# One order of products in all weight tiles of a pair, and all activation slots in one stretch of SBUF beside the split weights

## The chip, the cores and the metric

One NeuronCore of one Trainium2 chip. The metric is the device time of one execution in microseconds, the median of three runs. The profile is that of one further execution of the same program.

## What is computed

A two-layer encoder on 256 positions of 2048 channels. Layer 0 mixes by a conformer convolution module, layer 1 by differential attention; each is followed by a feed-forward network (FFN) with 5632 hidden channels and a short causal convolution in it. Everything is float32.

```python
for i in range(DEPTH):                                     # DEPTH = 2
    h = _rmsnorm(x, mix_norm[i])
    m = _conformer_conv(h, ...) if i % 2 == 0 else _diff_attention(h, ...)
    x = x + m
    h = _rmsnorm(x, ffn_norm[i])
    x = x + _conv_ffn(h, ffn_w_up[i], ffn_dw_w[i], ffn_dw_b[i], ffn_w_down[i])
return _rmsnorm(x, final_norm_g)

def _conv_ffn(h, w_up, dw_w, dw_b, w_down):
    u = _causal_dwconv(h @ w_up, dw_w, dw_b)
    gate, val = jnp.split(u, 2, axis=-1)
    return (jax.nn.silu(gate) * val) @ w_down
```

## The kernel before

Channels lie on the 128 partitions and the 256 positions along the free axis. Every matrix is walked in **pairs**: two column blocks of 128 outputs each (`j` = 0, 1), accumulated over all input blocks `k` of 128 channels into one PSUM tile of two banks (pool `pp`, two buffers, so that one pair is evacuated while the next is computed). Weights come by DMA on SP's queue in tiles of 128x1024 (four `k` of a pair, 512 KB) into pool `rawp`. `split_w` makes two tiles of each: `hi`, a rounded copy by ScalarE (L160), and `lo`, the rest, by VectorE or GpSimd (L164). An activation tile holds the same two parts side by side, 128x2x256.

`pair` issues, for each `k` and each `j`, two products on TensorE: **main**, the `hi` weights with both parts of the activation (512 columns), and **corr**, the `lo` weights with the activation's upper part (256 columns, added to the second half of the same bank). For all `k` but the last the order is main, corr (L249, L250); for the last `k` of a pair it is corr, main (L246, L247). One main with its corr is called a **duo** below; a pair over 16 `k` has 32 duos. A pair of FFN's `w_up` has 16 `k`; one of `w_down` has 8 (4 in the first of its chunks). `merged` pairs (the conv module's `w_in`, and the last pair of each `w_down`) use another form, three products of 256 columns (L240). When a pair is done, `post` sums the two halves and works on them on ScalarE and VectorE.

Activation tiles are slots of 2 KB a partition. `act_tile` gives them out of pool `acta` (25 slots) as long as it has one free, and after that out of `actb` (8 slots). The pools lie in SBUF in the order in which they are opened: `const`, `rawp`, `hip`, `lop`, `acta`, `sm`, and then `ph1`, which holds what only the convolution module needs. When `acta` first runs out, `ph1` is closed, and `ph2` (attention's tiles) and `actb` are laid over it. So the slots of `acta` lie behind the weight tiles at multiples of 2 KB, and those of `actb` 44,512 bytes behind the end of `acta`, which is no multiple of 64 bytes (32 over).

TensorE's order of instructions is fixed when the program is built. A planner runs through the program with modelled times and puts an instruction where its inputs are ready, by the order of the source among those that are. Between the duos come small blocks of other products: the norm's channel sums (`chan_sums`, L297, four of 2 columns) and its row broadcast (`rows`, L303, four of 128 columns), each once per norm, a few duos before and after a pair's end early in the FFN; the attention's scores, transposes and value products (L952, L977, L987, L1005) in the pairs of its heads; and single products of the bias table and of lambda (L839, L857) in the first FFN's first two pairs. Within an FFN no other block comes after the row broadcast, up to its last, merged pair. In `w_o` the first two pairs hold back their last `k` until attention's last head is done (`held`), so that the next pair begins without the swapped order there.

Of the kernel before, what the change touches and what calls it, by code (L numbers as in the profile page):

```python
# [8 lines left out]
F32 = mybir.dt.float32  # L9
# [5 lines left out]
P = 128  # L15
S = 256
# [3 lines left out]
FK = 3  # L20
# [5 lines left out]
class Cfg:  # L26


    def __init__(self, d, f, kc=4):
        self.D, self.F = d, f  # L30
        self.KT = d // P
        self.FT = f // P
        self.H = d // (2 * HD)
        self.KC = kc
        self.NW = kc * 256
        self.kcs = [(i, kc) for i in range(0, self.KT, kc)]
        full = self.KT // 2
        first = self.FT % full or full
        self.chunks = [(0, first)] + [(i, full) for i in range(first, self.FT, full)]
        self.VK = kc // 2  # L40
        self.NA, self.NB = self.KT + self.KT // 2 + 1, 8

        self.G = [3] * (self.KT - 3) + [5, 6, 0]

        self.ND = 16
# [16 lines left out]
class Builder:  # L62
    def __init__(self, ctx, tc, cfg, a):
        self.tc, self.nc, self.c, self.a = tc, tc.nc, cfg, a
        ec = ctx.enter_context
        self.ctx = ctx
        self.const = ec(tc.tile_pool(name="const", bufs=1))
        self.rawp = ec(tc.tile_pool(name="rawp", bufs=5))
        self.hip = ec(tc.tile_pool(name="hip", bufs=6))
        self.lop = ec(tc.tile_pool(name="lop", bufs=6))  # L70
        self.acta = ec(tc.tile_pool(name="acta", bufs=cfg.NA))
        self.sm = ec(tc.tile_pool(name="sm", bufs=2))
        self.pp = ec(tc.tile_pool(name="pp", bufs=2, space=bass.MemoryType.PSUM))
        self.px = ec(tc.tile_pool(name="px", bufs=1, space=bass.MemoryType.PSUM))
        self.dr = ec(tc.tile_pool(name="dr", bufs=1, space=bass.MemoryType.DRAM))
        self.ph1_stack = ExitStack()
        self.ph1 = self.ph1_stack.enter_context(tc.tile_pool(name="ph1", bufs=2))
        self.actb = None
        self.na, self.nb = cfg.NA, 0
        self.coloff, self.ncol = cfg.cols()  # L80
        self.steps, self.W, self.todo = [], [], {}
        self.s = self.n = self.np_ = self.ns = 0
        self.every = self.pool_first = None
# [4 lines left out]


    def b2(self, tag, dt=F32):  # L90
        return self.sm.tile([P, 2, S], dt, tag=tag, name=self.nm(tag), bufs={"E": 4, "Y": 4, "Z": 2, "A": 2}[tag])

    def b1(self, tag):
        return self.sm.tile([P, S], F32, tag=tag, name=self.nm(tag), bufs={"G": 4, "O": 3, "M": 3}[tag])
# [17 lines left out]


    def act_tile(self, dt=F32R):
        if self.na > 0:
            self.na -= 1
            return ("a", self.acta.tile([P, 2, S], dt, tag="act", name=self.nm("act")))
        if self.actb is None:
            self.ph1_stack.close()
            self.ph2 = self.ctx.enter_context(self.tc.tile_pool(name="ph2", bufs=1))  # L120
            self.actb = self.ctx.enter_context(self.tc.tile_pool(name="actb", bufs=self.c.NB))
            self.nb = self.c.NB
        assert self.nb > 0
        self.nb -= 1
        return ("b", self.actb.tile([P, 2, S], dt, tag="actb", name=self.nm("actb")))

    def free(self, tiles):
        for w, _ in tiles:
            if w == "a":
                self.na += 1  # L130
            else:
                self.nb += 1


    def load_w(self):
# [90 lines left out]
    def pair(self, wsrc, off, ksub, src, post, lo="v", pre=None, held=None, merged=False, halves=None):  # L226


        nc = self.nc
        box = {}  # L230
        first, last = ksub[0][0], ksub[-1][0] + ksub[-1][1] - 1

        def one(hi, lo_, kk, k):
            xt = src(k)[1]
            for j in range(2):
                ps = box["ps"][j] if halves else box["ps"][:, j, :]
                cs = slice(j * P, (j + 1) * P)
                if merged:
                    for n, (w, x) in enumerate(((hi, 0), (hi, 1), (lo_, 0))):
                        nc.tensor.matmul(ps[:, 0:S], w[:, kk, cs], xt[:, x, :], start=(k == first and n == 0),  # L240
                                         stop=(k == last and n == 2))
                    continue
                main = (ps, hi[:, kk, cs], xt.rearrange("p a s -> p (a s)"))
                corr = (ps[:, S:], lo_[:, kk, cs], xt[:, 0, :])
                if k == last:
                    nc.tensor.matmul(*corr, start=False, stop=False)  # L246
                    nc.tensor.matmul(*main, start=False, stop=True)  # L247
                else:
                    nc.tensor.matmul(*main, start=(k == first), stop=False)  # L249
                    nc.tensor.matmul(*corr, start=False, stop=False)  # L250

        for si, (k0, nk) in enumerate(ksub):
            n = nk * 256
            w = wsrc[off:off + P * n].rearrange("(p n) -> p n", p=P)
            off += P * n

            def mm(hi, lo_, k0=k0, nk=nk, si=si):
                if si == 0:
                    box["ps"] = halves() if halves else self.pp.tile([P, 2, 512], F32, tag="pp", name=self.nm("pp"))
                for kk in range(nk):  # L260
                    if held is not None and k0 + kk == last:
                        box["w"] = (hi, lo_, kk, last)
                    else:
                        one(hi, lo_, kk, k0 + kk)

            end = si == len(ksub) - 1
            self.step(w, n, 256, mm, post=(lambda: post(box["ps"])) if end and held is None else None,
                      pre=pre if si == 0 else None, lo=lo[si % len(lo)])
        if held is not None:
            held.append((lambda: one(*box["w"]), lambda: post(box["ps"])))  # L270
        return off
# [139 lines left out]
    def setup(self, n0):  # L411
        nc, c, a = self.nc, self.c, self.a
# [25 lines left out]
        with self.tc.manual_schedule(engines={ET.DVE, ET.Activation, ET.Pool}):  # L438
            for m in range(KT):
                if m in (0, 2):  # L440

                    first = self.split_w() if m == 0 else first
# [12 lines left out]

        self.todo[7] = [lambda: self.norm_cols(n0)]
        self.todo[8] = [lambda: self.norm_rows(n0)]
        self.fpad = []
        for i in range(2):
            t = self.const.tile([P, 2, S + FK - 1], F32, name=f"fpad{i}")  # L460
            nc.vector.memset(t[:, :, 0:FK - 1], 0.0)
            self.fpad.append(t)
        self.cpad = []
        for i in range(4):
            t = self.ph1.tile([P, S + CK + 1], F32, name=f"cpad{i}", bufs=1)
# [5 lines left out]
    def conv_module(self, nin, nout):  # L471
        c, a = self.c, self.a
# [197 lines left out]
        def layernorm():  # L670
# [24 lines left out]
            nc.vector.tensor_tensor(mr, mean, rc, ALU.mult)  # L695

            rp = [self.psx("s", [P, S]) for _ in range(2)]
            rs = self.b2("E")
            for x, v in enumerate((rc, mr)):
                self.rows(rp[x], v)  # L700
# [129 lines left out]
    def attn_setup(self):  # L830

        nc, c, a = self.nc, self.c, self.a
        H = c.H
        rb = self.ph2.tile([NB, H], F32, name="rb")
        self.tc.keep_in_program_order(nc.gpsimd.dma_start(rb, a["relb"]))
        oh = self.b2("Z").rearrange("p a s -> p (a s)")[:NB, :384]
# [327 lines left out]
```

## Time and profile before

| | |
|---|---|
| median of 3 runs | 2229.67 us (2228.4 to 2231.36) |
| the profiled execution | 2228.45 us |
| its span, first to last instruction | 2226.7 us |
| granted TensorE clock over the span | 0.997 |

How to read it: the span is what the trace covers; 1.75 us of the profiled execution's time lie around it. The profiled execution is 1.2 us below the median. A timeline row gives the start and the length of one instruction (or of a run of like ones, `x4`), its engine, its line and its tiles, output before the arrow. Matmuls are pipelined, so that a row's length reaches over the start of the next; what a product costs in a stream is the distance between two starts. Starts are given to 0.01 us, so a cadence is read over several duos. A windows row gives a stretch, its length, the busy time and the number of instructions of TensorE's matmuls, its weight loads, VectorE, ScalarE and GpSimd in it, and then TensorE's granted clock, the DMA share and GB/s.

### The profile page before, as it was taken

How to read it: one execution, taken by the hardware profiler on the slowest of the kernel's cores; microseconds unless marked ns; L12 is line 12 of the kernel's file. 1: busy time of each engine (PE TensorE's matmuls, PEld its weight loads, DVE VectorE, ACT ScalarE, POOL GpSimd, SP SyncE). 2: the span in 40 equal slices, each digit the busy share in tenths (PEclk: the TensorE clock that was granted, in tenths of full speed). 3: DMA queues.
4: the chain of work that ended last, by engine and by line, in shares of the span. 5: the costliest groups of instructions: out<-in, count | busy, mean ns of one | idle time of the engine just before them, and what ended most of it. 6: DMA issues, size and time to landing. Idle time of an engine off the chain costs nothing.

```text
span 2226.7 us, 34566 instructions
## 1 busy us (share of the span) xinstructions
PE 2202.7 (99%) x13274; PEld 1935.3 (87%) x13274; DVE 1629.1 (73%) x2482; ACT 1200.9 (54%) x1799; POOL 251.1 (11%) x175
## 2 busy tenths in 40 slices
PE   9999899999999999999999999999999999999998
PEld 8899788888888888888888888888888888888887
DVE  5888777787767677677687778767777677776774
ACT  5333555555555455555565555555555455554554
POOL 2987510000000000000100000100000000000002
PEclk9999999999999999999999999999999999999999
DMA  7876365666666656665655555556666566666652
GB/s 262 229 221 199 115 189 184 196 200 196 198 197 200 189 189 186 191 187 186 194 171 182 171 171 172 173 188 189 188 185 189 188 189 189 190 189 189 189 188 97
DMA packets 127317, 417.15 MB, mean 187 GB/s; under 512 B 14608, under 2 KB 28576, under 8 KB 127152
## 3 DMA queue, kind: packets, MB, share of 16 engines
q1 hardware_dynamic: 115584, 403.32, 58.2%
q10 hardware_dynamic: 11472, 11.54, 2.1%
q8 instruction: 104, 1.70, 0.3%
q14 instruction: 61, 0.50, 0.1%
q0 software_dynamic: 96, 0.08, 0.0%
HBM read 410.13 MB, written 7.33 MB: 187 GB/s over the span
## 4 chain that ended last, share of the span: by engine, by line
PE 95%; issue 2%; DVE 1%; POOL 1%; DMA 1%; ACT 0%; POOLq 0%; ACTq 0%
PE pp L249 49%; PE pp L250 25%; PE pp L240 6%; PE pp L247 4%; PE pp L246 2%; PE pp L900 1%; PE pp L902 1%; PE pp L901 1%; PE s L952 1%; PE s L542 1%; DMA R<-ud 1%; PE o L987 0%; POOL lo L164 0%; PE s L249 0%; DVE s L599 0%
## 5 line engine op out<-in xcount | busy, mean ns | idle before, releaser
L249 PE MATMUL pp<-act,hi 128*128 128x512 f32 x3902 | 1378.7, 395 | 1.6 <-ACT hi L160 1.1
L250 PE MATMUL pp<-act,lo 128*128 128x256 f32 x3902 | 1095.0, 281 | 0.0
L164 DVE TENSOR_TENSOR lo<-raw,hi 128x1024 fp32r<-128x1024 f32 (+1 forms) x693 | 849.8, 1228 | 286.7 <-ACT hi L160 285.2
L160 ACT CAST hi<-raw 128x1024 fp32r<-128x1024 f32 (+1 forms) x753 | 788.0, 1047 | 499.8 <-PE pp L249 190.9
L249 PEld LDWEIGHTS pp<-act,hi 128*128 128x128 f32 x3902 | 731.6, 187 | 161.5 <-ACT hi L160 1.4
L250 PEld LDWEIGHTS pp<-act,lo 128*128 128x128 f32 x3902 | 737.1, 189 | 9.8
L249 PE MATMUL pp<-actb,hi 128*128 128x512 f32 x856 | 306.9, 396 | 0.0
L250 PE MATMUL pp<-actb,lo 128*128 128x256 f32 x856 | 240.3, 281 | 0.0
L347 POOL TENSOR_TENSOR ssq<-ssq,Z 128x512 f32<-128x512 f32 x24 | 35.9, 1496 | 1549.1 <-ACT Z L343 1549.0
L249 PEld LDWEIGHTS pp<-actb,hi 128*128 128x128 f32 x856 | 160.6, 188 | 38.4 <-issue 0.6
L240 PE MATMUL pp<-act,hi 128*128 128x256 f32 x1024 | 188.5, 286 | 3.1 <-ACT act L290 1.9
L240 PEld LDWEIGHTS pp<-act,hi 128*128 128x128 f32 x1024 | 160.7, 193 | 9.4 <-issue 4.9
L277 ACT COPY E<-pp 128x512 f32<-128x512 f32 x104 | 60.9, 586 | 190.1 <-PE pp L247 190.1
L250 PEld LDWEIGHTS pp<-actb,lo 128*128 128x128 f32 x856 | 161.5, 189 | 0.2
L402 ACT COPY E<-pp 128x512 f32<-128x512 f32 x109 | 63.9, 586 | 170.3 <-PE pp L247 162.6
L279 DVE TENSOR_TENSOR E<-pp,E 128x512 f32<-128x512 f32 x104 | 71.9, 691 | 111.5 <-ACT E L277 111.5
L788 DVE SCALAR_TENSOR_TENSOR Y<-fpad,prm,Y 128x256 f32<-128x256 f32 x352 | 146.7, 477 | 0.0
L240 PE MATMUL pp<-act,lo 128*128 128x256 f32 x512 | 145.4, 284 | 0.3 <-DVE lo L164 0.3
L164 POOL TENSOR_TENSOR lo<-raw,hi 128x1024 fp32r<-128x1024 f32 x60 | 142.8, 2406 | 14.3 <-ACT hi L160 7.3
L404 DVE TENSOR_TENSOR x<-pp,x 128x512 f32<-128x512 f32 x101 | 69.7, 690 | 87.8 <-ACT E L402 87.4
L785 ACT ACTIVATE Y<-fpad,prm 128x256 f32<-128x256 f32 x176 | 96.3, 595 | 45.5 <-DVE fpad L781 45.5
L599 DVE SCALAR_TENSOR_TENSOR s<-cpad,cprm,s 128x256 f32<-128x256 f32 x182 | 85.2, 486 | 20.2 <-PE s L542 16.8
(214 smaller groups left out, 1846.9 us busy)
## 6 DMA issues: line engine op xcount, KB each, us to landing
raw<-in_w_up_dram SPq DMA_DIRECT2D x352, 512.0 KB, 3.7
raw<-in_w_down_dram SPq DMA_DIRECT2D x176, 512.0 KB, 3.7
raw<-in_w_qk_dram SPq DMA_DIRECT2D x64, 512.0 KB, 3.6
raw<-in_w_in_dram SPq DMA_DIRECT2D x63, 512.0 KB, 4.8
raw<-in_w_out_dram SPq DMA_DIRECT2D x32, 512.0 KB, 3.8
raw<-in_w_v_dram SPq DMA_DIRECT2D x32, 512.0 KB, 3.7
raw<-in_w_o_dram SPq DMA_DIRECT2D x32, 512.0 KB, 3.7
R<-ud ACTq DMA_DIRECT2D x52, 132.0 KB, 5.9
```

The costliest lines, as they stand in the source:

```text
L160: nc.scalar.copy(hi[:, p], raw[:, p])
L164: ins = eng.tensor_tensor(lo[:, p], raw[:, p], hi[:, p].bitcast(F32), ALU.subtract)
L240: nc.tensor.matmul(ps[:, 0:S], w[:, kk, cs], xt[:, x, :], start=(k == first and n == 0), stop=(k == last and n == 2))
L247: nc.tensor.matmul(*main, start=False, stop=True)
L249: nc.tensor.matmul(*main, start=(k == first), stop=False)
L250: nc.tensor.matmul(*corr, start=False, stop=False)
L279: nc.vector.tensor_tensor(t, ps[:, :, 0:S], cs, ALU.add)
L402: nc.scalar.copy(cs, ps[:, :, S:])
L404: nc.vector.tensor_tensor(x, ps[:, :, 0:S], x, ALU.add)
L599: nc.vector.scalar_tensor_tensor(acc, u[:, j:j + S], self.col("cw", i * CK + j), acc, ALU.mult, ALU.add)
L785: nc.scalar.activation(y[:, j, :], u[:, j, FK - 1:], AF.Identity, scale=self.col("fw", ch * FK + FK - 1), bias=self.col("fb", ch))
L788: nc.vector.scalar_tensor_tensor(y[:, j, :], u[:, j, q:q + S], self.col("fw", ch * FK + q), y[:, j, :], ALU.mult, ALU.add)
```

## The change

- `pair` issues main, then corr for every `k`, the last one too.
- `actb` is gone: `acta` has 33 slots (the 25 and the 8), and the pools are opened in the order `const`, `hip`, `lop`, `acta`, `rawp`, `sm`.
- To make room, the tiles E and A of `sm` and the two `fpad` tiles of `const` move to `ph2`. `ph2` is opened by the new function `second`, called in the conv module's layernorm before its E tile (`rs`). `fpad` is made in `attn_setup`, and its two small memsets run on GpSimd in place of VectorE.

```diff
@@ -38,7 +38,7 @@
         first = self.FT % full or full
         self.chunks = [(0, first)] + [(i, full) for i in range(first, self.FT, full)]
         self.VK = kc // 2
-        self.NA, self.NB = self.KT + self.KT // 2 + 1, 8
+        self.NA = self.KT + self.KT // 2 + 9
 
         self.G = [3] * (self.KT - 3) + [5, 6, 0]
 
@@ -65,18 +65,19 @@
         ec = ctx.enter_context
         self.ctx = ctx
         self.const = ec(tc.tile_pool(name="const", bufs=1))
-        self.rawp = ec(tc.tile_pool(name="rawp", bufs=5))
+
         self.hip = ec(tc.tile_pool(name="hip", bufs=6))
         self.lop = ec(tc.tile_pool(name="lop", bufs=6))
         self.acta = ec(tc.tile_pool(name="acta", bufs=cfg.NA))
+        self.rawp = ec(tc.tile_pool(name="rawp", bufs=5))
         self.sm = ec(tc.tile_pool(name="sm", bufs=2))
         self.pp = ec(tc.tile_pool(name="pp", bufs=2, space=bass.MemoryType.PSUM))
         self.px = ec(tc.tile_pool(name="px", bufs=1, space=bass.MemoryType.PSUM))
         self.dr = ec(tc.tile_pool(name="dr", bufs=1, space=bass.MemoryType.DRAM))
         self.ph1_stack = ExitStack()
         self.ph1 = self.ph1_stack.enter_context(tc.tile_pool(name="ph1", bufs=2))
-        self.actb = None
-        self.na, self.nb = cfg.NA, 0
+        self.ph2 = None
+        self.na = cfg.NA
         self.coloff, self.ncol = cfg.cols()
         self.steps, self.W, self.todo = [], [], {}
         self.s = self.n = self.np_ = self.ns = 0
@@ -88,7 +89,8 @@
 
 
     def b2(self, tag, dt=F32):
-        return self.sm.tile([P, 2, S], dt, tag=tag, name=self.nm(tag), bufs={"E": 4, "Y": 4, "Z": 2, "A": 2}[tag])
+        pool = self.ph2 if tag in "EA" else self.sm
+        return pool.tile([P, 2, S], dt, tag=tag, name=self.nm(tag), bufs={"E": 4, "Y": 4, "Z": 2, "A": 2}[tag])
 
     def b1(self, tag):
         return self.sm.tile([P, S], F32, tag=tag, name=self.nm(tag), bufs={"G": 4, "O": 3, "M": 3}[tag])
@@ -112,24 +114,17 @@
 
 
     def act_tile(self, dt=F32R):
-        if self.na > 0:
-            self.na -= 1
-            return ("a", self.acta.tile([P, 2, S], dt, tag="act", name=self.nm("act")))
-        if self.actb is None:
-            self.ph1_stack.close()
-            self.ph2 = self.ctx.enter_context(self.tc.tile_pool(name="ph2", bufs=1))
-            self.actb = self.ctx.enter_context(self.tc.tile_pool(name="actb", bufs=self.c.NB))
-            self.nb = self.c.NB
-        assert self.nb > 0
-        self.nb -= 1
-        return ("b", self.actb.tile([P, 2, S], dt, tag="actb", name=self.nm("actb")))
+        assert self.na > 0
+        self.na -= 1
+        return ("a", self.acta.tile([P, 2, S], dt, tag="act", name=self.nm("act")))
 
     def free(self, tiles):
-        for w, _ in tiles:
-            if w == "a":
-                self.na += 1
-            else:
-                self.nb += 1
+        self.na += len(tiles)
+
+    def second(self):
+
+        self.ph1_stack.close()
+        self.ph2 = self.ctx.enter_context(self.tc.tile_pool(name="ph2", bufs=1))
 
 
     def load_w(self):
@@ -242,12 +237,8 @@
                     continue
                 main = (ps, hi[:, kk, cs], xt.rearrange("p a s -> p (a s)"))
                 corr = (ps[:, S:], lo_[:, kk, cs], xt[:, 0, :])
-                if k == last:
-                    nc.tensor.matmul(*corr, start=False, stop=False)
-                    nc.tensor.matmul(*main, start=False, stop=True)
-                else:
-                    nc.tensor.matmul(*main, start=(k == first), stop=False)
-                    nc.tensor.matmul(*corr, start=False, stop=False)
+                nc.tensor.matmul(*main, start=(k == first), stop=False)
+                nc.tensor.matmul(*corr, start=False, stop=(k == last))
 
         for si, (k0, nk) in enumerate(ksub):
             n = nk * 256
@@ -455,11 +446,6 @@
 
         self.todo[7] = [lambda: self.norm_cols(n0)]
         self.todo[8] = [lambda: self.norm_rows(n0)]
-        self.fpad = []
-        for i in range(2):
-            t = self.const.tile([P, 2, S + FK - 1], F32, name=f"fpad{i}")
-            nc.vector.memset(t[:, :, 0:FK - 1], 0.0)
-            self.fpad.append(t)
         self.cpad = []
         for i in range(4):
             t = self.ph1.tile([P, S + CK + 1], F32, name=f"cpad{i}", bufs=1)
@@ -695,6 +681,7 @@
             nc.vector.tensor_tensor(mr, mean, rc, ALU.mult)
 
             rp = [self.psx("s", [P, S]) for _ in range(2)]
+            self.second()
             rs = self.b2("E")
             for x, v in enumerate((rc, mr)):
                 self.rows(rp[x], v)
@@ -831,6 +818,11 @@
 
         nc, c, a = self.nc, self.c, self.a
         H = c.H
+        self.fpad = []
+        for i in range(2):
+            t = self.ph2.tile([P, 2, S + FK - 1], F32, name=f"fpad{i}")
+            nc.gpsimd.memset(t[:, :, 0:FK - 1], 0.0)
+            self.fpad.append(t)
         rb = self.ph2.tile([NB, H], F32, name="rb")
         self.tc.keep_in_program_order(nc.gpsimd.dma_start(rb, a["relb"]))
         oh = self.b2("Z").rearrange("p a s -> p (a s)")[:NB, :384]
```

## Rows read from the trace of the kernel before

**Rows 1.** Page, part 1: TensorE busy us, share of the span, instructions.

```profile
PE 2202.7 (99%) x13274; PEld 1935.3 (87%) x13274; DVE 1629.1 (73%) x2482; ACT 1200.9 (54%) x1799; POOL 251.1 (11%) x175
```

**Rows 2.** Timeline, a pair of the second w_up, then one of the first.

```profile
1496.88 0.39 PE L249 MATMUL pp<-act,hi 128*128 128x512 f32 x1
...
1505.55 0.39 PE L249 MATMUL pp<-actb,hi 128*128 128x512 f32 x1
...
660.12 0.39 PE L249 MATMUL pp<-actb,hi 128*128 128x512 f32 x1
...
664.34 0.28 PE L246 MATMUL pp<-actb,lo 128*128 128x256 f32 x1
...
665.04 0.40 PE L249 MATMUL pp<-act,hi 128*128 128x512 f32 x1
```

**Rows 3.** Timeline, first w_down: the last product of three pairs of 16 duos.

```profile
1000.10 0.40 PE L247 MATMUL pp<-act,hi 128*128 128x512 f32 x1
...
1005.66 0.39 PE L247 MATMUL pp<-act,hi 128*128 128x512 f32 x1
...
1011.30 0.40 PE L247 MATMUL pp<-act,hi 128*128 128x512 f32 x1
```

**Rows 4.** Timeline, w_out: the last product of pairs of 32 duos.

```profile
281.76 0.39 PE L247 MATMUL pp<-act,hi 128*128 128x512 f32 x1
...
292.87 0.39 PE L247 MATMUL pp<-act,hi 128*128 128x512 f32 x1
...
338.07 0.39 PE L247 MATMUL pp<-act,hi 128*128 128x512 f32 x1
```

**Rows 5.** Timeline, w_o: accumulator changes (pp, s) without a swapped order.

```profile
1401.14 0.40 PE L249 MATMUL pp<-act,hi 128*128 128x512 f32 x1
...
1403.26 0.40 PE L249 MATMUL s<-act,hi 128*128 128x512 f32 x1
...
1408.04 0.39 PE L249 MATMUL s<-act,hi 128*128 128x512 f32 x1
...
1409.43 0.39 PE L249 MATMUL pp<-act,hi 128*128 128x512 f32 x1
```

**Rows 6.** Timeline around the row broadcast, first FFN, then second FFN.

```profile
363.28 0.61 PE L303 MATMUL o<-ident,rc 128*128 128x128 f32 x4
...
363.64 0.36 PE L250 MATMUL pp<-act,lo 128*128 128x256 f32 x1
...
364.20 0.40 PE L249 MATMUL pp<-act,hi 128*128 128x512 f32 x1
...
365.94 0.39 PE L249 MATMUL pp<-act,hi 128*128 128x512 f32 x1
...
1486.56 0.60 PE L303 MATMUL o<-ident,rc 128*128 128x128 f32 x4
...
1486.92 0.47 PE L249 MATMUL pp<-act,hi 128*128 128x512 f32 x1
...
1487.35 0.39 PE L249 MATMUL pp<-act,hi 128*128 128x512 f32 x1
...
1488.76 0.40 PE L249 MATMUL pp<-act,hi 128*128 128x512 f32 x1
```

**Rows 7.** Timeline, attention: a block of six products and the duos behind it.

```profile
1216.54 0.83 PE L987 MATMUL o<-act,at 128*128 128x128 f32 x6
...
1217.56 0.40 PE L249 MATMUL pp<-act,hi 128*128 128x512 f32 x1
...
1218.95 0.40 PE L249 MATMUL pp<-act,hi 128*128 128x512 f32 x1
```

**Rows 8.** Windows, FFNs behind the row broadcast: us, busy us (instructions) per engine.

```profile
363.92:1073.26 709.34, 709.34 (x4063) 621.28 (x4062) 527.64 (x709) 393.38 (x538) 7.44 (x5) 1.00 0.62 193
1487.20:2207.68 720.48, 720.48 (x4120) 630.16 (x4119) 522.32 (x698) 395.14 (x539) 7.13 (x5) 1.00 0.59 183
```

**Rows 9.** Waits in the layernorm: total us, times, longest us.

```profile
ACT E L731 <- DVE act L708: 6.6, 1, 6.6
```

## The prediction

> **What bounds the kernel now.** The page's first part comes first: TensorE is busy for 2202.7 of the span's 2226.7 us, VectorE for 73%, ScalarE for 54% [rows 1]. So there are 24 us of idle TensorE in all. The list of TensorE's waits puts them at the start, in the layernorm and in the last norm; inside the two FFNs none stands. The granted clock is 1.00 of full speed (2.4 GHz) in both FFNs [rows 8]. Then only two things can move the time: how many products there are, which stays, and how fast they follow one another. So the view to read is TensorE's timeline, start against start.
>
> There the reader is to see that one duo (main and corr) does not have one price. In a long run of the second w_up, 25 duos on `acta` tiles take from 1496.88 to 1505.55, 8.67 us, 0.3468 us each [rows 2]. I call that the **short cadence**. In w_out, four pairs of 32 duos take from 292.87 to 338.07, 45.20 us, 0.3531 us each: the **long cadence**; the pair before them, with the same shapes, takes 11.11 us, 0.3472 [rows 4]. Nothing waits in either, and no shape differs. In the rows between, the distances are even in the short cadence and repeat over three duos in the long one, for as long as nothing disturbs them. So the cadence is something that TensorE keeps up, with a difference of 0.0063 us a duo, or 1.8%. What changes it is the question.
>
> Three things change it in the trace. **First, the swapped order at a pair's end.** In w_down two pairs of 16 duos take 5.56 and 5.64 us, and so on in turn through the whole phase: short, long, short [rows 3]. Between them lies nothing but the swapped last `k`. The swap itself costs nothing: its two duos take 0.70 us, from 664.34 to 665.04 [rows 2]. **Second, the step from `acta` to `actb` tiles.** In w_up the last `k` have their tiles in `actb`; the short cadence ends there, and the 12 duos from 660.12 to 664.34 take 4.22 us, 0.3517 each [rows 2]. After the swap the next pair begins with the short one again. **Third, blocks of other products.** After the row broadcast of the first FFN, which ends on a corr, 5 duos take 1.74 us: short. After that of the second FFN, which ends on a main, 4 duos take 1.41 us, 0.3525: long [rows 6].
>
> What does not change it is the pair's end as such. In w_o, where held pairs leave the swap out, the long cadence goes on through a change of pair and accumulator (6 duos from 1401.14 to 1403.26, 2.12 us, 0.3533), and the short one through another change of accumulator (4 duos, 1.39 us) [rows 5].
>
> **The change part by part.** *One order.* It removes the switch at every pair's end. By rows 5 the cadence then goes on from pair to pair. *One stretch.* It removes the second switch. From the shapes of the tiles, `hip`, `lop` and `acta` keep their distances (24 KB each), and all move down by 24,640 bytes, a multiple of 64; so the 25 old slots should behave as before, and the 8 new ones like them. Within an FFN no switch is left after the row broadcast. So each FFN runs in one cadence from there to its last pair, some 700 us at one rate.
>
> The price of each: behind the row broadcast the first FFN has 4063 matmuls in 709.34 us, which is 2030 duos (and the first products of the merged pair), 0.3494 a duo; the second has 4120 in 720.48 us, 2059 duos, 0.3499 [rows 8]. All short, the first is 2030 x 0.3468 = 704.0 us, 5.3 less; all long, 2030 x 0.3531 = 716.8 us, 7.5 more. The second: 714.1 us, 6.4 less, or 727.0 us, 6.5 more. In w_out the pair that ends at 292.87 follows a wait for weights and is short; the wait stays, so the cadence stays short through the four pairs behind it: 128 x 0.0063 = 0.8 us less. Attention and w_o have 16 x 32 + 8 x 32 = 768 duos with blocks in nearly every pair; they stay a mixture, taken at 0, with bounds at half of 768 x 0.0063 on either side, 2.4 us.
>
> Which cadence? In the first FFN the row broadcast is followed by a corr, and the duos behind it are short [rows 6]. The cadence was short before it too, though, and in the changed kernel it may be long there, since the block of L857, which is followed by a main, leaves the long one, and the swap that ended it is gone. The blocks of eight products in w_o that end on a corr turn the long cadence short, those of one or two in attention do not; I take the four of the broadcast with the long ones. In the second FFN the broadcast is followed by a main, and the cadence is long before and after it. But the changed kernel comes to it otherwise: the channel sums ahead of it are followed by a corr, and no swap follows them, so the short cadence should reach the broadcast. For a short cadence broken by a block that is followed by a main there are near rows: six products of L987, then 4 duos in 1.39 us, short [rows 7], one of three such places, all alike. I take the short one in both. The planner may move a block by one product, which is the main uncertainty.
>
> *The rest at nothing.* `second` opens `ph2` before `rs`: ScalarE's copy into it (L731) now also waits until the readers of `ph1` are done. It already waits 6.6 us for VectorE [rows 9], and the last taps are over before that; behind it on ScalarE stand the layernorm's activations, for which TensorE waits, so that without this cover each us would be a us of the total. I take 0, between 0 and 0.2. The two `fpad` memsets of four elements a partition leave VectorE's start and stand on GpSimd ahead of the table's DMAs and the norm's power, on an engine busy for 11% of the span [rows 1]: 0, with 0.1 either way. The last `k` now needs the activation's lower part one product earlier, at most 0.12 us, and only where that part is just made: in w_out's first pairs, whose next step waits for weights in any case, and in w_o, where it is there some us earlier. 0. In the short cadence a weight tile (8 duos) is used up in 2.77 us in place of up to 2.82; in the FFNs VectorE is busy for 527.64 of 709.34 us and ScalarE for 393.38 [rows 8], so both follow, and the DMA share is 0.62.
>
> The sum against the profiled execution: 2228.45 - 5.3 - 6.4 - 0.8 = 2215.95, with 2.4 either way. The median shown is 1.2 us above that execution, so the forecast is 2217.2, from 2214.8 to 2219.6.
>
> **The rivals.** *One FFN takes the long cadence.* If the broadcast of the second FFN hands on the long cadence as it does now [rows 6], its 6.5 us eat what the first one gives: 2228.45 - 5.3 + 6.5 - 0.8 = 2228.85; the other way round, 2228.45 + 7.5 - 6.4 - 0.8 = 2228.75. With the 1.2 us, 2230, from 2227.5 to 2232.5. For it speaks that the second FFN's broadcast is the one place of its kind and the cadence is long behind it; against it, rows 7.
>
> *Both take the long one.* What decides is the product that follows the row broadcast, and the run that reaches it. If the long cadence behind L857 passes the first broadcast, and the second one keeps its own, nothing in 700 us turns either back, where the swap now does so at every second pair: 2228.45 + 7.5 + 6.5 - 0.8 = 2241.65, median 2242.9. This is the slower case. Against it speaks that it needs both.
>
> *The change doesn't do what it says:* the cadence hangs on neither order nor slot, and the mixture stays: 2229.7. Against it are rows 2 and 3; for it, that I cannot say from the trace why a swapped order shifts the cadence, and that all addresses move. The Trainium skill has a rule on its side: SBUF — State Buffer, section "Who interferes with whom", gives TensorE two independent read ports, one for the moving operand and one for the weights, and says that it never waits on anyone. By that rule no slot is better than another, and a duo's price would be one. The trace does not agree: 0.3468 us on `acta` and 0.3517 on `actb` in the same loop [rows 2].
>
> **How the numbers follow.** Both short 0.45; one long 0.30; both long 0.18; no effect 0.07. The predicted time is that of the first, 2217.2. The range takes in the first, the second and the fourth with their bounds, 0.82 of the chance: 2213 to 2234; both long is left out. The likeliest case alone is 2214.8 to 2219.6. Within 0.2% (4.5 us) is about what a measurement of this kernel cannot tell from no change. So faster is 0.45, the same 0.37 (the second and fourth), slower 0.18.
>
> **What would show it.** In the changed trace: no product on the old lines of the swapped order; in w_down, pairs of 16 duos all alike, 5.55 us each if short, 5.65 if long, in place of turns; in w_up no step within a pair; the window behind the row broadcast 704 or 717 us in the first FFN and 714 or 727 in the second. The prediction is wrong if a pair's end changes the cadence without the swap, if cadences other than these two appear because all addresses have moved, or if the block in front of an FFN's long stretch leaves the long cadence.

## The result, and the profile after

| | before | after |
|---|---|---|
| median | 2228.9 us (6 runs, 2226.8 to 2231.4) | 2240.6 us (6 runs, 2237.3 to 2249.6) |
| ratio, 95% interval | | 1.0053 [1.0042, 1.0063] |
| profiled execution, its span | 2228.45, 2226.7 us | 2240.56, 2238.8 us |

The change makes the kernel slower by half a per cent. The first part of the page after answers to [rows 1]:

```profile
PE 2208.4 (99%) x13274; PEld 1936.4 (86%) x13274; DVE 1639.7 (73%) x2480; ACT 1194.2 (53%) x1799; POOL 250.3 (11%) x177
```

TensorE is busy for 5.7 us more with the same 13274 products, and idle for 30.4 us of the span in place of 24.0. So there are two effects: the products follow one another more slowly, and there are new waits. Between marks that both kernels have (the first product behind each FFN's row broadcast, the first product of its merged pair) the 12.1 us lie as follows, in us. The last column is a later run, which holds copies ahead of casts.

| stretch | before | after | difference | copies first |
|---|---|---|---|---|
| start to the first broadcast's end | 363.6 | 368.4 | +4.7 | 366.3 |
| FFN 0 | 709.5 | 717.4 | +7.9 | 704.0 |
| between the FFNs | 413.8 | 416.9 | +3.1 | 416.5 |
| FFN 1 | 720.6 | 716.9 | -3.7 | 714.0 |
| the end | 19.2 | 19.2 | 0.0 | 20.0 |

After has the second broadcast five duos later, which shifts 1.7 us from FFN 1 to the stretch ahead of it. The windows of after that answer to [rows 8]:

```profile
368.66:1085.92 717.26, 716.18 (x4063) 621.81 (x4062) 533.31 (x709) 390.09 (x539) 5.57 (x5) 1.00 0.62 191
1502.97:2219.75 716.78, 715.67 (x4110) 627.91 (x4109) 524.50 (x697) 390.19 (x538) 7.81 (x5) 1.00 0.60 184
```

The granted clock is 1.00 in both, as before, and TensorE's busy time is now 1.1 us short of each window: something waits inside the FFNs, where nothing waited before.

**The new waits.** The list of TensorE's waits (total us, times, longest us) has these rows, of which before has only the third, with 0.4 us:

```profile
PE pp L240 <- DVE x L395: 3.1, 3, 1.5
...
PE pp L240 <- DVE x L398: 2.5, 1, 2.5
...
PE pp L240 <- DVE act L711: 1.9, 2, 1.5
```

L395 and L398 are the additions that empty an accumulator of `pp`: TensorE stands because both accumulators are full. They stand where a pair is short or comes after a stop: in w_out, in the first chunk of each w_down (pairs of 8 duos) and behind the held pairs of w_o. The third row is the wait for the activation's lower part at the start of w_out; both runs of the next section have it too. The timeline shows why. First, before, the end of the last w_up pair ahead of FFN 0's first w_down:

```profile
474.60 0.39 PE L247 MATMUL pp<-actb,hi 128*128 128x512 f32 x1
...
475.02 0.59 ACT L277 COPY E<-pp 128x512 f32<-128x512 f32 x1 [1.85 <-PE pp L247]
...
475.51 1.05 ACT L160 CAST hi<-raw 128x1024 fp32r<-128x1024 f32 x1
...
475.64 0.69 DVE L279 TENSOR_TENSOR E<-pp,E 128x512 f32<-128x512 f32 x1 [1.21 <-ACT E L277]
```

With the swapped order the last product is a main, and it frees two things at once: the accumulator, and the `hi` slot. It ends at 474.99, ScalarE copies at 475.02, and the next cast follows. Now the same place after:

```profile
478.49 0.39 PE L240 MATMUL pp<-act,hi 128*128 128x512 f32 x1
...
478.72 0.28 PE L241 MATMUL pp<-act,lo 128*128 128x256 f32 x1
...
478.96 1.05 ACT L155 CAST hi<-raw 128x1024 fp32r<-128x1024 f32 x1 [1.42 <-issue]
...
479.92 0.58 ACT L268 COPY E<-pp 128x512 f32<-128x512 f32 x1
...
480.05 1.23 DVE L159 TENSOR_TENSOR lo<-raw,hi 128x1024 fp32r<-128x1024 f32 x1 [1.21 <-ACT hi L155]
...
481.19 0.68 DVE L270 TENSOR_TENSOR E<-pp,E 128x512 f32<-128x512 f32 x1
...
481.50 0.28 PE L241 MATMUL pp<-act,lo 128*128 128x256 f32 x1
...
481.93 0.50 PE L240 MATMUL pp<-act,hi 128*128 128x512 f32 x1 [0.15 <-DVE E L270]
```

The last main ends at 478.88 and frees the `hi` slot one product before the pair is done (479.00). So the planner finds the next cast ready first and puts it ahead of the copy; on VectorE the `lo` of that cast goes ahead of the addition in the same way. The copy starts 0.92 us behind the pair's end in place of 0.03, the addition 2.19 us in place of 0.65, and it ends at 481.87, when the next pair of 8 duos (2.77 us) is already over. In ScalarE's program order, 211 of the 213 copies stand behind exactly one cast more than before. In pairs of 16 and 32 duos the second accumulator hides that.

**The cadence.** The swap's turns [rows 3] and the `actb` step [rows 2] are gone, as predicted, and a cadence now lasts for hundreds of us. Windows of 75 us of after (columns as in [rows 8]; 434 or 435 products is the short cadence, 426 or 427 the long one, with no wait in any of the four):

```profile
400.00:475.00 75.00, 75.00 (x434) 66.11 (x433) 57.42 (x83) 42.84 (x61) 0.00 (x0) 1.00 0.64 198
520.00:595.00 75.00, 75.00 (x427) 65.01 (x426) 55.39 (x80) 41.48 (x60) 0.00 (x0) 1.00 0.64 194
...
1510.00:1585.00 75.00, 75.00 (x426) 64.97 (x426) 56.81 (x82) 42.34 (x60) 0.00 (x0) 1.00 0.63 189
1660.00:1735.00 75.00, 75.00 (x435) 66.14 (x434) 57.43 (x82) 42.83 (x62) 0.00 (x0) 1.00 0.61 190
```

FFN 0 is short up to the wait that ends at 481.9 us. In the pairs of 8 duos behind it each late accumulator can tip the rate again: long, short from 497.8, and from 503.7 long to the FFN's end. The last of these hold-ups is in no list of waits. The addition that empties the accumulator ends at 503.30; the main at 503.45 is the first of a pair, and its corr comes 247 ns behind it in place of 230:

```profile
503.45 0.41 PE L240 MATMUL pp<-act,hi 128*128 128x512 f32 x1
503.69 0.28 PE L241 MATMUL pp<-act,lo 128*128 128x256 f32 x1
```

FFN 1 is long from its broadcast to the wait that ends at 1633.4, once more from 1639.4 to 1645.4, and short from there on. The broadcast itself, in the timeline:

```profile
1500.25 0.39 PE L240 MATMUL pp<-act,hi 128*128 128x512 f32 x1
...
1501.98 0.39 PE L240 MATMUL pp<-act,hi 128*128 128x512 f32 x1
1502.21 0.28 PE L241 MATMUL pp<-act,lo 128*128 128x256 f32 x1
1502.33 0.61 PE L294 MATMUL o<-ident,rc 128*128 128x128 f32 x4
...
1503.13 0.39 PE L240 MATMUL pp<-act,hi 128*128 128x512 f32 x1
...
1504.90 0.40 PE L240 MATMUL pp<-act,hi 128*128 128x512 f32 x1
```

Five duos take 1.73 us ahead of it (0.346 each) and 1.77 us behind it (0.354).

### The profile page after: what moved, and what is told of

It reads as the page before. It is cut to its first block, busy times and chain, and to the rows that moved or that the text cites. A ratio compares the mean times of both kernels' runs of the same rounds, so it can differ in the third digit from the quotient of the medians.

```text
span 2238.8 us, 34599 instructions
## 1 busy us (share of the span) xinstructions
PE 2208.4 (99%) x13274; PEld 1936.4 (86%) x13274; DVE 1639.7 (73%) x2480; ACT 1194.2 (53%) x1799; POOL 250.3 (11%) x177
## 4 chain that ended last, share of the span: by engine, by line
PE 86%; DVE 1%; ACT 0%; issue 0%; POOL 0%; POOLq 0%; DVEq 0%; ACTq 0%
PE pp L240 53%; PE pp L241 27%; PE pp L894 1%; PE pp L893 1%; PE pp L892 1%; PE s L944 1%; PE pp L235 1%; PE o L979 0%; ACT hi L155 0%; DVE lo L159 0%; PE s L240 0%; PE t L969 0%; DVE x L395 0%; PE s L241 0%; PE t L997 0%
## 5 line engine op out<-in xcount | busy, mean ns | idle before, releaser
L240 PE MATMUL pp<-act,hi 128*128 128x512 f32 x5184 | 1822.8, 396 | 8.0 <-DVE x L395 3.1
L241 PE MATMUL pp<-act,lo 128*128 128x256 f32 x5184 | 1454.2, 281 | 0.0
L240 PEld LDWEIGHTS pp<-act,hi 128*128 128x128 f32 x5184 | 972.2, 188 | 239.3 <-DVE x L395 5.6
L241 PEld LDWEIGHTS pp<-act,lo 128*128 128x128 f32 x5184 | 979.2, 189 | 1.7 <-issue 0.6
L235 PEld LDWEIGHTS pp<-act,hi 128*128 128x128 f32 x1024 | 161.6, 194 | 9.8 <-issue 4.9
L235 PE MATMUL pp<-act,lo 128*128 128x256 f32 x512 | 146.0, 285 | 0.0
L235 PEld LDWEIGHTS pp<-act,lo 128*128 128x128 f32 x512 | 99.3, 194 | 0.4 <-issue 0.4
L400 DVE TENSOR_TENSOR x<-x,E 128x512 f32<-128x512 f32 x109 | 75.2, 691 | 3.2
L395 DVE TENSOR_TENSOR x<-pp,x 128x512 f32<-128x512 f32 x101 | 69.1, 684 | 6.8 <-ACT E L393 6.8
L768 DVE TENSOR_TENSOR fpad<-E,rstd 128x512 f32<-128x512 f32 x88 | 60.8, 692 | 2.9
L893 PE MATMUL pp<-lo,act 128*128 128x512 f32 x128 | 50.8, 397 | 0.0
```

Of the source, the lines that this page charges most:

```text
L241: nc.tensor.matmul(*corr, start=False, stop=(k == last))
L395: nc.vector.tensor_tensor(x, ps[:, :, 0:S], x, ALU.add)
L400: nc.vector.tensor_tensor(x, x, cs, ALU.add)
L893: nc.tensor.matmul(o, xt[:, 0, ts], lo[:, kk, :], start=False, stop=False)
```

## The experiments

My theory, before the first of them: the waits come from the new order alone, through the copies' place on ScalarE, and they cost twice, once as idle time and once by the cadence that they leave behind. The rival: the new places of the pools do it.

### The order alone, and the pools alone

The first is the kernel before with one order; the second is the kernel after with the old swap put back.

```diff
-                if k == last:
-                    nc.tensor.matmul(*corr, start=False, stop=False)
-                    nc.tensor.matmul(*main, start=False, stop=True)
-                else:
...
+                nc.tensor.matmul(*main, start=(k == first), stop=False)
+                nc.tensor.matmul(*corr, start=False, stop=(k == last))
```

> Kernel before with the one order of products alone; pools as before. Theory: it is the order that puts every evacuation copy on ScalarE (E from pp) behind one more weight tile's hi cast, so TensorE waits for VectorE's x add at the starts of the short w_down pairs, in w_out and in w_o, 6 us in all, as in the changed kernel; the steps between acta and actb stay, so w_up pairs keep about 0.3484 us a duo: 2229 + 6 = 2235, 2231 to 2241. Rival (the pools bring the waits): no such wait, 2229 within 4.

> Changed kernel with the old swapped order at a pair's last k; new pools. Theory: no added wait; without the step to actb a w_up pair of 32 duos that begins in the long cadence ends in it and hands it on over the swap (as the four w_out pairs before did), so nearly all w_up pairs take 11.30 us in place of 11.17: 84 x 0.13 = 11 us, 2240, 2236 to 2243; w_down pairs still in turns of 5.56 and 5.64. Rival (slots change nothing): 2229 within 4.

The order alone: 2232.2 us, ratio 1.0012 [1.0003, 1.0022]. It has the same waits on the additions (3.1 and 2.5 us) and the same one cast ahead of the copies. The pools alone: 2241.3 us, ratio 1.0054 [1.0039, 1.0069], no such wait, and the copies where they were. So the waits belong to the order. But the pools alone cost as much as the whole change, by the cadence: a window of its w_up,

```profile
520.00:595.00 75.00, 75.00 (x427) 65.18 (x426) 54.84 (x80) 42.59 (x60) 0.00 (x0) 1.00 0.62 197
```

is long in spite of a swap at each pair's end; before had 432 there. What brought the short cadence back in w_up shows in the timeline of the order alone, where no swap is left, but `actb` is:

```profile
536.29 0.40 PE L245 MATMUL pp<-act,hi 128*128 128x512 f32 x1
...
542.54 0.39 PE L245 MATMUL pp<-actb,hi 128*128 128x512 f32 x1
...
547.47 0.40 PE L245 MATMUL pp<-act,hi 128*128 128x512 f32 x1
```

18 duos on `acta` tiles take 6.25 us (0.347 each), the 14 behind them on `actb` tiles 4.93 (0.352), and the next pair is short again. So it goes at 101 of this run's 102 returns from `actb` to `acta` in the two FFNs. The duos on `actb` settle into turns of 346 and 361 ns, also where they are reached in the long cadence (508.97 us), and these turns stand on no `acta` tile of the 14 profiles. So the return to `acta` tiles brings the short cadence back by itself, and not the swap, as I had read [rows 2]. With the swap beside it, before, the duos behind a return were short at all 42 places in FFN 0, but at only 38 of 59 in FFN 1. The one stretch of slots took this return away.

### The copies ahead of the casts again

After, with each cast held behind the copy that stood ahead of it before (212 of the 213 copies have their old place again):

```diff
-            nc.scalar.copy(hi[:, p], raw[:, p])
+            with self.tc.issue_after(self.evac) if self.evac else ExitStack():
+                nc.scalar.copy(hi[:, p], raw[:, p])
+            self.evac = self.evac2
...
-        nc.scalar.copy(cs, ps[:, :, S:])
+        self.evac2 = nc.scalar.copy(cs, ps[:, :, S:]).ins
```

> Changed kernel, with the hi casts on ScalarE held behind the evacuation copies so that ScalarE has the order of the kernel before. Theory: no wait of TensorE for the x add; so no change of cadence inside an FFN; first FFN short, 704 us behind the row broadcast, second FFN long, 727 us (its row broadcast stands behind a corr): 2228.5 - 5.3 + 6.5 - 0.8 = 2229, 2226 to 2233. Rival (the cadence changes by itself in 700 us): a change within an FFN without a wait at that place, 2234 and varying from run to run.

The waits of the order go, all but one (of 3.1 and 2.5 us, 1.5 stays, behind the held pairs of w_o). The median is 2234.1 us, ratio 1.0028 [1.0013, 1.0042], but the ten times fall into three groups: 2222.6; seven from 2231.6 to 2238.0; 2242.9 and 2243.7. The profiled execution is the first, and both of its FFNs are short from end to end:

```profile
366.59:1070.49 703.90, 703.90 (x4063) 620.57 (x4062) 527.51 (x709) 393.68 (x538) 7.42 (x5) 1.00 0.60 194
1487.14:2200.97 713.83, 713.83 (x4120) 628.43 (x4119) 522.26 (x698) 395.32 (x539) 7.12 (x5) 1.00 0.57 185
```

The steps between the groups fit zero, one or two long FFNs, some 11 us each; of this program only the first group was profiled. The expectation was missed: the median lies 1 us above its range, and the profile has FFN 1 short, where I had it long behind its broadcast. Its broadcast was reached long and left the short cadence.

### Idle products that set the cadence

The kernel above, with eight idle identity products between a main and its corr in the fourth w_up pair of each FFN. They interrupt the stream for 1.78 us (16 instructions in the trace), twice what I expected.

```diff
+                if kick and k == first + 8 and j == 0:
+                    idle = self.psx("t", [P, P])
+                    for _ in range(8):
+                        i = nc.tensor.matmul(idle, self.ident, self.ident, start=True, stop=True)
```

> As e3_evac_first, and in the fourth w_up pair of each FFN eight extra products of 128 columns (identity with identity, result unused) between a main and its corr, 0.9 us each time. Theory: such a block that ends on a corr leaves the short cadence whatever came before, and nothing changes it afterwards: both FFNs short from there, 2216 + 2 x 0.9 = 2218, 2215 to 2221. Rival (a block does not set the cadence): as e3_evac_first plus 2 us, 2231.

2224.6 us, ratio 0.999 [0.9971, 1.0009], in two groups: seven from 2220.9 to 2225.8, three from 2235.7 to 2237.7: above the range expected, by the blocks' price and by the second group. FFN 1 comes out of its broadcast long and is short from the block to its end. The profiled execution is of the second group, and its timeline shows what I had missed:

```profile
488.01 0.68 DVE L405 TENSOR_TENSOR x<-pp,x 128x512 f32<-128x512 f32 x1
...
488.67 0.28 PE L251 MATMUL pp<-act,lo 128*128 128x256 f32 x1
...
488.79 0.46 PE L242 MATMUL pp<-act,hi 128*128 128x512 f32 x1
```

The addition ends at 488.69; the main at 488.79 needs that accumulator, and the corr behind it comes after 295 ns in place of 230. This hold-up of 65 ns is in no list of waits, and FFN 0 is long from there to its end, 596 us. So pairs of 8 duos have next to no slack with the old order of copies either.

### Where the interruption stands

Is it the product behind which TensorE was interrupted that decides?

> The kernel of the run with copies ahead of casts, with a block of eight idle identity products at four places in the middle of a w_up pair: FFN 0, pair 4, behind a corr; FFN 0, pair 21, between a main and its corr; FFN 1, pair 4, between main and corr; FFN 1, pair 21, behind a corr. Theory: what a stretch takes up is decided by the product after which TensorE was held up: behind a main the short cadence follows (346.7 ns a duo), behind a corr the long one (353.4). Then FFN 0 goes short to long at its first block (about 386 us) and long to short at its second, and FFN 1 short (or long) to short at its first and short to long at its second. Rival 1: any interruption draws a cadence anew, by chance: the four places come out in no order. Rival 2: a block always leaves the short cadence: all four stretches are short. The time itself tells little (by the theory some 2231 to 2236).

The blocks stand at 382, 644, 1520 and 1780 us (one run, 2235.5 us). Windows between them:

```profile
400.00:475.00 75.00, 75.00 (x426) 65.08 (x425) 56.07 (x82) 42.91 (x61) 0.00 (x0) 1.00 0.60 193
...
660.00:735.00 75.00, 75.00 (x434) 66.14 (x434) 56.60 (x82) 43.43 (x62) 0.00 (x0) 1.00 0.63 201
...
1530.00:1605.00 75.00, 75.00 (x434) 66.14 (x434) 56.88 (x82) 43.05 (x61) 0.00 (x0) 1.00 0.60 188
1640.00:1715.00 75.00, 75.00 (x426) 64.99 (x426) 54.73 (x77) 41.04 (x57) 0.00 (x0) 1.00 0.59 187
1790.00:1865.00 75.00, 75.00 (x435) 65.55 (x434) 56.80 (x82) 42.95 (x61) 0.00 (x0) 1.00 0.60 189
```

Behind a main both come out short. Behind a corr the first turned short to long, but the last, against the theory, long to short (it had been turned long by a hold-up of 64 ns at 1624.6, in w_down). So behind a corr, at these two places, the cadences were exchanged. The row broadcasts of the 14 profiles, looked at afterwards, agree in the main. FFN 0's, behind a main, left the short cadence in all. FFN 1's, behind a corr in all, made long of short four times and short of long seven times; two (before, and the pools alone) reach it in the long cadence only four duos behind a swap, and left it once long and once short; and one reached it in turns of 343 and 350 ns, the short rate on average, and kept them. So it is no rule for every block: the six products of [rows 7], behind a corr, left the short cadence as it was.

### One product, and other addresses

One idle product in w_up pairs 4 and 14 of each FFN, with the copies first and then in the changed kernel itself; and the changed kernel with 32 bytes of pad ahead of the weight tiles.

```diff
+        pad = self.const.tile([P, 8], F32, name="pad")
+        nc.vector.memset(pad, 0.0)
```

> The kernel of the run with copies ahead of casts, with one idle identity product between a main and its corr in pairs 4 and 14 of w_up of each FFN (pair 14 is the second behind the short w_down pairs, where the run with eight products was turned to the long cadence in 3 of 10 executions). Theory: a single product turns a stretch as eight did, and the second one mends what the short w_down pairs turn: both FFNs run at 346.7 ns a duo in every execution, 2219 us (2216 to 2223), with all executions within some 4 us of each other. Rival: one product is too small an interruption: the time is drawn as in the run without blocks, 2222 to 2244 with a median near 2234.

> The changed kernel, its order of casts and copies untouched, with one idle identity product between a main and its corr in pairs 4 and 14 of w_up of each FFN. It keeps the waits on the accumulators (about 6 us) and takes away only the long cadence behind them. Theory: FFN 0 runs long from its first w_down pairs to the block in pair 14 only, and FFN 1 from its row broadcast to the block in pair 4: 2240.6 - (1073 - 520) x 6.7 / 353.4 - (1632 - 1530) x 6.7 / 353.4 = 2228 us (2225 to 2231). Rival: the cadence is not what costs, or one product doesn't turn it: 2240.

> The changed kernel with a pad of 32 bytes a partition ahead of the pools, so that hi, lo and the activation slots start at multiples of 64 bytes and not 32 bytes beside them. Theory of the slot addresses: if the bytes at which the operands start decide the cadence, every duo gets a new one, and the time leaves 2240 by some 10 us or more in either direction, with neither 346.7 nor 353.4 ns a duo. Rival: only the alternation of products and the interruptions decide: 346.7 and 353.4 again, 2240 us (2236 to 2244).

With the copies first: 2223.9 us, ratio 0.9979 [0.9962, 0.9997], five of six from 2220.2 to 2224.8 and one at 2233.6, so not every execution was short as expected. In the changed kernel: 2247.6 us (4 runs, 2241.3 to 2251.6), ratio 1.0077, a miss by 20 us. In the profiled one (2244.0) the product at 522 us turned FFN 0 from short to long, and the one at 1530 did so in FFN 1: one product may tip the cadence either way. The pad: 2239.3 us, ratio 1.004 [1.0028, 1.0052], and the two cadences are 346.7 and 353.3 ns as without it; its profiled execution (2228.4) is one in which FFN 0 stayed short behind its waits:

```profile
520.00:595.00 75.00, 75.00 (x435) 66.14 (x434) 56.27 (x81) 42.74 (x61) 0.00 (x0) 1.00 0.64 200
1510.00:1585.00 75.00, 75.00 (x427) 65.02 (x426) 57.41 (x82) 41.60 (x60) 0.00 (x0) 1.00 0.59 188
```

So 32 bytes in the place of all operands together decide nothing here. The pad doesn't move the activations against the weights, which is how the slots of `actb` lay apart.

### The two costs apart

Three blocks of eight, at the same places, in the kernel with the copies first and in the changed kernel.

> The kernel of the run with copies ahead of casts, with a block of eight idle identity products between a main and its corr at three places: w_up pair 14 of FFN 0 (behind its short w_down pairs), pairs 4 and 14 of FFN 1. Theory: eight products behind a main left the short cadence at all four places looked at so far, so both FFNs run at 346.7 ns a duo in every execution, but for at most 35 us behind each interruption (0.7 us at the worst); with three blocks of 1.78 us: the profiled time of the run with copies ahead of casts in which both FFNs were short, 2222.6, + 5.3 = 2228 us (2224 to 2230), all executions within some 4 us. Rival: four of four was chance, and the cadence is drawn at each block: two or three clusters, up to 2244.

> The changed kernel, its order of casts and copies untouched, with the same three blocks of eight. Theory: the blocks take away the long cadence, the waits on the accumulators stay: 6.4 us over the run that has the same blocks and the copies ahead of the casts, 2234.5 us (2230 to 2237), all executions within some 4 us. Rival: cadence drawn at each block, as with one product: 2241 to 2252. Rival 2: the waits cost nothing beyond the cadence that they turn: as the other run, 2228.

Measured: 2227.3 us (11 runs, 2225.8 to 2230.4), ratio 0.999 [0.9981, 0.9999], and 2234.7 us (9 runs, 2234.0 to 2236.6), ratio 1.0022 [1.0013, 1.0032]. Both groups are about as narrow as expected. In both profiles each block left the short cadence, also where the short w_down pairs had turned it long. The two lists of waits differ in the additions; the first is that with the copies first:

```profile
PE pp L251 <- DVE x L412: 1.5, 1, 1.5
```

```profile
PE pp L249 <- DVE x L410: 3.0, 3, 1.5
PE pp L249 <- DVE x L413: 2.5, 1, 2.5
```

So the place of the copies is worth 2234.7 - 2227.3 = 7.4 us. Between the two spans it is 7.7, of which 4.4 are idle TensorE and 2.1 lie in each FFN. The long cadence in the changed kernel is an estimate from medians of two sets of runs: 2240.6 - (2234.7 - 3 x 1.78) = 11.2 us. Together they make 18.6 us; 2240.6 less that is 2222.0, near the best execution with the copies first (2222.6), in which both FFNs were short.

### A version that beats both

Four products cost half of eight. First behind FFN 0's short pairs and early in FFN 1, then behind the short pairs of both (copies first in each):

```diff
+                                      block="main" if i == 13 else None)
```

> Copies ahead of casts, with a block of four identity products between a main and its corr at two places: w_up pair 14 of FFN 0 and pair 4 of FFN 1. Theory: four products turn a stretch as eight do, at half the cost: 2222.6 + 2 x 0.9 = 2224 us (2220 to 2226), faster than before by 0.25% or more. Rival: four are as unreliable as one: 2222 to 2244 in clusters, median near 2232.

> Copies ahead of casts, with a block of four idle identity products between a main and its corr in w_up pair 14 of each FFN, right behind the short w_down pairs: in the run with four products at pairs 14 and 4 both blocks left the short cadence, and only the short w_down pairs of FFN 1 (1618.4 us), with no block behind them, turned it to long. Theory: with a block behind the short w_down pairs of both FFNs, both run at 346.7 ns a duo but for some 30 us behind each of these; 2222.6 + 2 x 0.9 + 2 x 0.6 = 2225 us (2221 to 2227), in every execution, faster than before by 0.2 to 0.3%. Rival: what turned the times of the run with four products to 2232 to 2237 in 9 of 12 executions was that four products are as unreliable as one: clusters between 2222 and 2244, median near 2232.

The first: 2234.3 us, ratio 1.001 [0.9997, 1.0023], three runs from 2221.8 to 2225.2 and nine from 2232.6 to 2236.9. Both of its blocks left the short cadence; it was a hold-up in the short w_down pairs of FFN 1 (1618.4 us), with no block behind it, that turned it long. So the expectation missed by the place of the block, not by its size. The second: 2223.3 us (11 runs, 2221.7 to 2227.6), ratio 0.9979 [0.997, 0.9988], faster than before by 0.2% and than the change by 0.8%. In its profile FFN 1 was turned long at 1613.4 and is short again behind the block at 1644.8:

```profile
520.00:595.00 75.00, 75.00 (x435) 66.14 (x434) 58.31 (x85) 44.39 (x63) 0.00 (x0) 1.00 0.60 196
...
1660.00:1735.00 75.00, 75.00 (x435) 66.14 (x434) 56.41 (x79) 42.47 (x61) 0.00 (x0) 1.00 0.59 190
```

## Why the prediction was wrong

**What held.** TensorE's pace is the whole of the time. Without swap and step a cadence lasts for hundreds of us, and its price was right: for all short I had 704.0 and 714.1 us, and with the copies first, when both were short, the stretches took 704.0 and 714.0. "No effect" has fallen.

**The step that failed** is "Within an FFN no switch is left after the row broadcast." I had asked what the order does to TensorE's stream and where each operand must be ready, but not what the last product of a pair frees, and in which order. The copy of the accumulator stood in no term of the sum; I had set "the rest" at nothing without naming it. Its price is 7.4 us, and the late accumulators are themselves the switches: between 481.9 and 503.7 us, in the pairs of 8 duos of FFN 0's first w_down, they turned the stretch that I had at 704.0 us long, and it took 717.4. That such a pair leaves 2.77 us in which to empty an accumulator, against 5.55 and 11.1 in pairs of 16 and 32 duos, was there to be worked out.

**The second step that failed** is "I take the short one in both." FFN 1's broadcast came behind a corr as in [rows 6], and the short cadence reached it as I had said, but it left the long one. I had set [rows 7], six products of another kind, above the one place of its own kind. The rows could not have told more, since before reached that place in the long cadence. In 11 of the 14 profiles the broadcast exchanges the two; why is open.

**A reading that was half right**: that after the swap the next pair is short again. The swap does turn the cadence pair by pair in w_down [rows 3]. In w_up, with the pools alone changed, it hands on the long one, and with the order alone changed the return to `acta` tiles brings the short one without a swap. So the one stretch removed not only the step into the long cadence, as I had counted, but also what ended it. My reading came from the first FFN; in the second, before, 21 of 59 pairs began long.

**The rest.** For w_out I had -0.8 us and for the start nothing; with the copies first that stretch still takes 2.7 us more than before, and the one between the FFNs 2.7 us more, where I had 2.4 as the bound. A wait of 1.5 us on the additions behind w_o's held pairs is in the second, and 1.7 us more on the activation's lower part (2.1 in place of 0.4) in the first; I did not take these apart further. The wait for the lower part, which I had at 0, is some 1.5 us at the start of w_out in this run and in the changed kernel, and 1.2 with the pools alone, so that the order of the products is not its only cause. For the move of E, A and `fpad` no new row shows in TensorE's waits.

**The rival nearest in number**, both FFNs long at 2242.9, is not what happened: FFN 1 was long for some 136 of 717 us, and the waits, which that rival doesn't have, fill the difference. By the rule of the Trainium skill that I had weighed (SBUF — State Buffer, "Who interferes with whom") no slot is better than another. The pad doesn't speak against it; the duos on `actb` do (0.3517 us before, 0.352 with the order alone), and their turns of 346 and 361 ns follow the slots and not the cadence in which they are reached. What it is in these slots is open: no run moved the activations alone.

## What to carry to other kernels

The order of the last products of an accumulation also sets the order in which their operands and the accumulator come free, and a scheduler that takes what is ready first will follow it: look at what then stands ahead of the evacuation, and measure the slack in the shortest accumulation, not in the usual one. Where one engine runs at 99% on one kind of work, take its pace from distances between starts over long stretches, and ask of every interruption, tens of ns too, which pace follows it. Time such a kernel in many executions and look at the groups: ten executions of one program lay up to 21 us apart here (2222.6 to 2243.7).

## What was not expected of the hardware

- The stream of mains and corrs has two steady rates, 346.7 and 353.3 ns a duo (in the long one 349, 350 and 361 ns in turn, on `actb` tiles 346 and 361), at the same granted clock of 1.00, with no wait, for up to 714 us. I know of no row that shows what differs inside.
- A hold-up of 65 ns changed the rate of the next 596 us, one of 17 ns in the changed kernel that of the next 582. Hold-ups of 60 to 70 ns at such places left either rate.
- Four or eight idle products between a main and its corr left the short rate at 14 of 14 places, 9 of them reached in the long one; one product left the long rate at 2 of 8. Behind a corr, the four products of the broadcast, or eight idle ones, exchanged the rates at 13 of the 16 places, among them all that were reached well settled in the even short cadence or in the long one.
- Added work can therefore pay: two blocks of four products, some 0.9 us each, took 2234.1 us to 2223.3, by not letting a long stretch stand.
